# A decoder step on one core: two scattered stores on another queue, a head norm on VectorE, earlier gathers and weight splits, and memory scores three steps ahead

## The chip, the core and the metric

The kernel runs on one core of one Trainium2 chip. The core has a matrix engine (TensorE, PE in the profile), a vector engine (VectorE, DVE), an activation engine (ScalarE, ACT), a general engine (GpSimd, POOL) and an engine that here only issues transfers (SyncE, SP). Each engine works through its own queue in order. SP, ACT and POOL can each issue DMA transfers; the profile calls the issuing side SPq, ACTq, POOLq. Operands lie in SBUF; PE writes its sums to PSUM, which has eight banks of 128 x 512 floats.

The metric is the time on the device of one execution, in microseconds. The kernel before took 1546.40, 1548.47 and 1551.26 us in three runs, 1548.47 us in the median.

## The reference: what is computed

One layer of a hybrid decoder for a prompt of 1024 tokens and for 8 single sample tokens with their caches, all in float32 and width 1024:

```python
hp = rmsnorm(xp, norm_mix[l])
qa, ka, va, qr, kr, vr, gr = project(hp, w_in[l])
oa = diff_attention_prompt(qa, ka, va, rel_bias, lam)
s_p, o_r = retention_prompt(rotary(qr, pos_p), rotary(kr, pos_p) * kr_scale, vr, lg)
xp = xp + merge_groups(oa, o_r, gr, subln_a[l], lam_init) @ w_out[l]
mk_p, mv_p = mem_kv(mem_prompt, norm_mem_kv[l], w_mk[l], w_mv[l])
xp = xp + mem_attend(rmsnorm(xp, norm_mem_q[l]), mk_p, mv_p, w_mq[l], w_mo[l])
xp = xp + sq_relu_mlp(rmsnorm(xp, norm_mlp[l]), w_up[l], w_down[l])
...
k_past = cache_k[l][page_table].reshape(Bd, past, H_A, 2 * DK_A)
oa_d = diff_attention(qa_d, k_all, v_all, pos_d, kpos_d, rel_bias, lam)
```

Four heads of differential attention are each divided by their own root mean square (`head_rms`) before the output projection; four retention heads are run in chunks of 128 tokens. The memory attention has four heads of width 256 over 256 memory tokens. The sample tokens take the same path, with keys and values gathered from pages of a cache.

## The kernel before, in words

Every product of two float32 matrices is made of three matmuls, on a high part and a low part of each operand (high x high, high x low, low x high). A weight "unit" of 128 x 1024 is loaded by SP into a ring of three raw buffers (`raw`, L103), its high part is a cast on ACT (`wh`, L109) and its low part a subtraction on DVE or POOL (`wl`, L110). Activations are held transposed in `UH` and `UL` (high and low), 8 row tiles by 1032 columns (1024 prompt tokens and 8 sample tokens).

The order of the work is set by three things. The program is written in the order of its stages. A planner then orders each engine's queue by that program order and by when it believes an instruction's inputs are ready. And `pin` holds PE to the written order where it is set, while `issue_after(x)` puts instructions behind instruction x on x's engine.

The stages, with the stretch of the profile that each takes:

- To 56 us: the retention queries and keys (`qkp`, 8 PSUM banks at once), and the factors 1/rms of the 1032 tokens (`rstd`, a power on POOL, L121). L219 and L220 store these factors to a row in DRAM (`rrow`), one 4-byte element at a time, 1032 of them. ACT then takes the eight banks out (`qk`, L320), and the retention values (`vrp`) begin. Their weights are four units (`raw_u`, split into `vrw` for the first two).
- To 250 us: retention, chunk by chunk, and the attention values `va`. What one chunk leaves is turned into an operand by `pend()`, that is `to_operand`: four transposes on PE (`trR`), a cast, a subtraction and two stores. The last chunk's `pend()` runs at t = 0 of the loop over `va`.
- To 455 us: the attention heads, a loop over g, ten steps a head (x = g mod 10). A step has one `turn` (transposes `trA` of the weights `e`, L70), one `weigh` (L67) and, at some x, `scores` of later tiles; projections of the next head (`qkp`) fill PE's queue as long as there are any, and after them the sample tokens' scores (`dsc`) on gathered cache pages (`ck`, an indirect DMA of POOL, L577, into the same ring of three raw buffers). The norm of a finished head h-1 is spread over later steps: `norm_sums` at x = 2, `norm_factors` at x = 3 (column sums `ct`, three small products, and the power on POOL), `norm_send` at x = 4, `norm_row` at x = 5 (transpose `hrT`, a store and a broadcast load `rbh`), `norm_out` at x = 7: for heads 0 and 1 four products of 128 x 256 on POOL (L828) and a store, for head 2 one product on DVE (L831).
- To 566 us: the output projection `pr_o` over pairs (ft, c) through seven PSUM banks, with the gathered cache values of the sample tokens accumulated on DVE beside it (`dacc`, L1218). `fetch(2)` and `fetch(3)`, at (3,0) and (4,1), ask for weight units 4 to 7 (`who`, `wlo`); each also loads two rows of the residual.
- To 700 us: the memory queries (`mq`), the first two heads of memory keys (`mk`, taken out by L1395, `mko`) and the memory values (`mv`). Keys and values go to DRAM and come back as one unit a head (`raw_kv`, `wh_kv`, `wl_kv`).
- To 775 us: the memory attention, a loop over t of 16 pairs of query tiles, four a head. Step t has `scores` of pair t+2 (`ms`; a minimum `mmn` L1463 on DVE, two exponentials L1467 on ACT, a reciprocal, two scalings `me` L1471 on DVE), `weights` of pair t+1 (transposes `mtr`, cast `mph` L1482 on ACT, subtraction `mpl` L1483 on DVE) and `values` of pair t (`mpv`; cast `UH` L1501 on ACT, subtraction `UL` L1502 on DVE). The keys of heads 2 and 3 are PE's filler in it (`mk_units`, `mem_keys`, 48 matmuls each). Banks: `sp` 3, `pv` 2, `tr` 1, and two for the filler.
- To 1551 us: the memory output projection, the up projection and the down projection, both by a seven-product scheme. The change does not touch them.

Of the kernel before, what the change touches and what calls it, by code (L numbers as in the profile page):

```python
# [2 lines left out]

# [7 lines left out]
F32 = mybir.dt.float32  # L11
# [8 lines left out]
P = 128  # L20
D = 1024
NT = 1024
ND = 8
T = NT + ND
# [24 lines left out]
def decoder_step(ctx: ExitStack, tc: tile.TileContext, i: dict, o: dict):  # L49
    nc = tc.nc  # L50
# [110 lines left out]
    seen = {}  # L161
    s_ps = ExitStack()
    PS0 = s_ps.enter_context(pool("s_ps", space=PSUM))
    with pool("s") as A:
# [54 lines left out]
        nc.sync.dma_start(rrow[0:1, :NT].rearrange("a (t p) -> p (a t)", p=P), rstd1[:, :8])  # L219
        nc.sync.dma_start(rrow[0:1, NT:].rearrange("a p -> p a"), rstd1[:8, 8:9])  # L220


        lp = A.tile([P, 4, 64], F32, tag="lp", name="lp")
# [16 lines left out]
    with pool("a") as A:  # L240
# [267 lines left out]
        for t in (8, 0, 1, 2, 3, 4, 5, 6, 7):  # L508
            if t == 4:

                opd = [PS.tile([P, 512], F32, tag="op", name=f"opd_{x}", bufs=2) for x in range(2)]
                for p in range(2):
                    for x in range(2):
                        mm(opd[x][:4, :], hsel[:, p, :], wvs[p][:, 4 * x : 4 * x + 4, :], p == 0, p == 1)
                od = A.tile([P, 8, P], F32, tag="sn", name="od").rearrange("p s v -> p (s v)")[:4, :]
                for x in range(2):
                    nc.scalar.copy(od[:, x * 512 : x * 512 + 512], opd[x][:4, :])
                nc.sync.dma_start(ord_, od.rearrange("h (s v) -> h s v", s=8))
                odt = A.tile([P, 512], F32, tag="t1", name="odt", bufs=2)
                nc.sync.dma_start(odt[:8].rearrange("s (h v) -> s h v", h=4), ord_[:, :, :].rearrange("h s v -> s h v"))  # L520
                head_norm_gate(odt, gate_d, 8, 8, gate_d)
            if t == 0:
                with tc.issue_after(seen["PE"]):
                    pend()
            if t == 6:
                with tc.issue_after(seen["PE"]):
                    to_operand(gate_d, 8, 8, "d")
            ps, n = tokproj(units, t, f"vap_{t}", PS) if t < 8 else (decproj(units, f"vap_{t}", PS, vdec[:8]), 8)
            seen["PE"] = nc.cur_bb.bb.instructions[-1]
            v = vdec if t == 8 else A.tile([P, 512], F32, tag="gate", name=f"va_{t}", bufs=2)  # L530
            nc.scalar.activation(v[:n], ps[:n], AF.Copy, scale=rstd1[:n, t : t + 1])
            nc.sync.dma_start(o["v_p"][t * P : t * P + n, :] if t < 8 else o["v_s"], v[:n])
# [69 lines left out]
    with pool("b") as A:  # L602
# [171 lines left out]
        def norm_factors(h, sq):  # L774
# [48 lines left out]
        def norm_out(h):  # L823
            oraw, rbh = oraws[h], rows[h]
            if h < 2:
                for x in range(4):
                    xs = slice(x * 256, x * 256 + 256)
                    nc.gpsimd.tensor_mul(oraw[:, xs], oraw[:, xs], rbh[:, xs])  # L828
                nc.sync.dma_start(OP[h, :, :NT], oraw)
            else:  # L830
                nc.vector.tensor_mul(oraw, oraw, rbh)  # L831
                split_gain(oraw, subln8, h, 0, NT, gcol=0)
# [183 lines left out]
        for g in range(-4, 40):  # L1016
# [37 lines left out]
            if h > 0:  # L1054
# [54 lines left out]
    def proj_residual(A, bank, base, ktorder, xsrc, xdst, ssum, nm, us0, steps, when, parts, ahead=0, early=None, stage=()):  # L1109
# [167 lines left out]
    with pool("d") as A:  # L1277
# [97 lines left out]
        def head_kv(h):  # L1375
# [5 lines left out]
                     o["mv"][:, h * 256 : h * 256 + 256].rearrange("(x p) v -> p x v", p=P)),  # L1381
                ]

            KV[h] = unit_of(kv, f"kv{h}", lo_engine=nc.gpsimd if h else None)

        def mem_keys(pr, ps, us):
            for f in range(2):
# [8 lines left out]
                mo.rearrange("p (f m) -> p f m", f=2), ps.rearrange("p (f m) -> p f m", f=2),  # L1396
                rmb.unsqueeze(1).to_broadcast([P, 2, 256]),
            )
            nc.sync.dma_start(
                o["mkT"][pr * 256 : pr * 256 + 256, :].rearrange("(f p) m -> p f m", p=P), mo.rearrange("p (f m) -> p f m", f=2))  # L1400

# [47 lines left out]
        def scores(h, tp):  # L1449
            qh, ql = QS[h]  # L1450
            kvh, kvl = KV[h]
            sp = PS.tile([P, 2, 256], F32, tag="sp", name=f"ms_{h}_{tp}", bufs=3)
            for x in range(2):
                tk = slice((2 * tp + x) * P, (2 * tp + x) * P + P)
                mm3(
# [3 lines left out]
                        for f in range(2)  # L1459
                    ],  # L1460
                )
            mn = A.tile([P, 2], F32, tag="mmn", name=f"mmn_{h}_{tp}", bufs=2)
            nc.vector.tensor_reduce(mn, sp, AX.X, ALU.min)  # L1463
            sm = A.tile([P, 2], F32, tag="msm", name=f"msm_{h}_{tp}", bufs=2)
# [9 lines left out]
        def weights(h, tp):  # L1474
# [5 lines left out]
            ph = A.tile([P, 512], F32R, tag="mph", name=f"mph_{h}_{tp}", bufs=2)  # L1480
            pl = A.tile([P, 512], F32R, tag="mpl", name=f"mpl_{h}_{tp}", bufs=2)
            nc.scalar.copy(ph, tr)  # L1482
            nc.vector.tensor_sub(pl, tr, ph.bitcast(F32))  # L1483
# [33 lines left out]
        head_q(0)  # L1517
        us_mo = []
        pin[0] = True
        for t in range(-2, 16):  # L1520
            if t == -2:
                us = mk_units(2, None)
                fill = mem_keys(2, PD.tile([P, 512], F32, tag="mk", name="mk_2", bufs=1), us)
            if t == -1:
                head_kv(1)
                head_q(1)
            if t == 3:
                us = mk_units(3, nc.gpsimd)
                fill = mem_keys(3, PD.tile([P, 512], F32, tag="mk", name="mk_3", bufs=1), us)
            if t == 4:  # L1530
                head_kv(2)
                head_q(2)
            if t == 8:
                head_q(3)
            if t == 9:
# [8 lines left out]
            if t == -1:  # L1544
# [8 lines left out]
            if t in (2, 7):  # L1553
                for _ in fill:
                    pass
            if t in (14, 15):
# [658 lines left out]
```

## Time and profile before

| | before |
|---|---|
| median of three runs | 1548.47 us |
| the profiled execution | 1553.3 us |
| its span, first to last instruction | 1551.5 us |
| mean granted TensorE clock | 0.988 |
| PE busy | 1494.2 us, 96% |
| DVE busy | 1072.6 us, 69% |
| ACT busy | 651.0 us, 42% |
| POOL busy | 440.8 us, 28% |

The profiled execution is 4.8 us above the median. Several views of it are used below. The list of waits gives, for an engine and a line, what it stood idle for, the idle time in total, how often, and the longest. The table of stretches gives an engine's busy time and number of instructions in a stretch, then the granted clock of TensorE (1.00 is full), the share of the DMA engines that was busy, and GB/s. The timeline gives start, length, engine, line, operation, what it writes from what it reads, shapes and count, and behind them in brackets the idle time before it and what ended it. The chain of waits follows the work that ended last back through whatever released each piece. A tile's own view gives for each line the shortest, middle and longest duration in ns and the first and the last start in us. Matmuls are pipelined, so a busy PE is not PE at its peak, but an idle PE is idle.

### The profile page before, as it was taken

What the parts mean: (1) busy time and instruction counts of PE and PEld (TensorE: products, weight loads), DVE (VectorE), ACT (ScalarE), POOL (GpSimd) and SP (SyncE); (2) the same over time, 40 slices, a digit from 0 to 9 for tenths busy, and PEclk for the clock granted to TensorE, in tenths of its full rate; (3) what the DMA queues carried; (4) which work ended last, traced back from release to release, by engine and by line L of the source; (5) the groups of instructions that cost most, each with busy time, mean ns of one, the idle gap of its engine ahead of it and who ended that gap; (6) DMA issues with size and microseconds to landing.
All of it is one profiled execution on the core that took longest, in us unless ns stands there. A gap on an engine that the chain in (4) does not pass through costs nothing.

```text
span 1551.5 us, 26774 instructions
## 1 busy us (share of the span) xinstructions
PE 1494.2 (96%) x10483; PEld 1394.0 (90%) x10483; DVE 1072.6 (69%) x2096; ACT 651.0 (42%) x1267; POOL 440.8 (28%) x461
## 2 busy tenths in 40 slices
PE   9899999999999899999999899999999899999997
PEld 7678869999759899988899899999999799999996
DVE  4324513988865735566696988888788688787887
ACT  6323323665642332046634643333334444334454
POOL 0343302122533421124222234443335402020360
PEclk9999999999999999999999999999999999999999
DMA  8645334212766156451583334434335873636313
GB/s 291 171 116 156 78 104 115 82 51 69 235 215 240 48 202 180 138 183 64 182 269 129 101 138 151 151 138 150 137 138 172 293 232 86 197 82 198 96 42 110
DMA packets 121874, 230.02 MB, mean 148 GB/s; under 512 B 14209, under 2 KB 74480, under 8 KB 121620
## 3 DMA queue, kind: packets, MB, share of 16 engines
q1 hardware_dynamic: 91508, 170.30, 35.3%
q0 software_dynamic: 21024, 41.10, 8.6%
q10 hardware_dynamic: 9216, 16.91, 2.9%
q8 instruction: 82, 1.34, 0.4%
q14 instruction: 44, 0.36, 0.1%
HBM read 168.93 MB, written 57.52 MB: 146 GB/s over the span
## 4 chain that ended last, share of the span: by engine, by line
PE 63%; DVE 17%; DMA 11%; ACT 4%; issue 3%; POOL 1%; SPq 0%; DVEq 0%; ACTq 0%; POOLq 0%
PE dn L1928 17%; PE Z L1778 5%; PE mq L67 5%; PE pr_o L67 4%; PE qkp L67 4%; PE Y L1778 4%; PE vrp L67 3%; PE vap L67 3%; DVE wu L1617 3%; PE grp L67 3%; DMA raw_up<-in_wall 3%; PE X L1778 2%; PE pr_m L67 2%; PE sp L67 2%; PE av L67 2%
## 5 line engine op out<-in xcount | busy, mean ns | idle before, releaser
L1928 PE MATMUL dn<-UH,wd 128*128 128x258 f32 x1792 | 326.1, 284 | 7.7 <-ACT wd L1906 4.3
L1928 PEld LDWEIGHTS dn<-UH,wd 128*128 128x128 f32 x1792 | 278.2, 190 | 9.2 <-ACT wd L1906 4.7
L1928 PE MATMUL dn<-UL,wd 128*128 128x258 f32 x896 | 253.3, 283 | 0.0
L1928 PEld LDWEIGHTS dn<-UL,wd 128*128 128x128 f32 x896 | 169.7, 189 | 0.1
L1804 ACT ACTIVATE hq<-r 128x258 f32<-128x258 f32 x128 | 53.5, 419 | 162.8 <-DVE r L1803 162.8
L2008 DVE TENSOR_TENSOR c<-c,dn 128x258 f32<-128x258 f32 x216 | 88.4, 418 | 35.5 <-PE dn L1928 33.4
L1778 PE MATMUL Z<-T_h,wu 128*128 128x258 f32 x512 | 100.0, 287 | 7.0 <-DVE u L1828 5.3
L1906 ACT CAST wd<-raw_d 128x512 fp32r<-128x512 f32 x96 | 58.9, 618 | 102.6 <-PE dn L1928 84.5
L1617 DVE TENSOR_TENSOR wu<-raw_up,wu 128x512 fp32r<-128x512 f32 x96 | 92.0, 959 | 9.2 <-ACT wu L1616 9.2
L1778 PE MATMUL X<-UH,wu 128*128 128x258 f32 x512 | 97.7, 282 | 0.4 <-ACT p L1825 0.4
L110 DVE TENSOR_TENSOR wl_u<-raw_u,wh_u 128x1024 fp32r<-128x1024 f32 x46 | 59.8, 1308 | 50.9 <-ACT wh_u L109 49.0
L1778 PEld LDWEIGHTS Z<-T_h,wu 128*128 128x128 f32 x512 | 81.4, 189 | 10.4 <-DVE u L1828 8.3
L1907 DVE TENSOR_TENSOR wd<-raw_d,wd 128x512 fp32r<-128x512 f32 x96 | 75.5, 790 | 14.3 <-ACT wd L1906 14.2
L1778 PEld LDWEIGHTS X<-UH,wu 128*128 128x128 f32 x512 | 81.3, 188 | 0.7 <-ACT p L1825 0.7
L1900 DVE TENSOR_TENSOR UL<-raw_h,UH 128x1032 fp32r<-128x1032 f32 x56 | 77.3, 1381 | 6.4 <-ACT UH L1899 6.4
L109 ACT CAST wh_u<-raw_u 128x1024 fp32r<-128x1024 f32 x50 | 52.3, 1050 | 69.9 <-PE mq L67 43.2
L1899 ACT CAST UH<-raw_h 128x1032 fp32r<-128x1032 f32 x56 | 58.8, 1055 | 52.0 <-PE dn L1928 30.9
L1810 POOL TENSOR_TENSOR ht<-hq 128x258 f32<-128x258 f32 x32 | 22.3, 698 | 202.1 <-ACT hq L1804 188.1
L1920 POOL TENSOR_TENSOR raw_d<-raw_d,raw_d 128x512 f32<-128x512 f32 x16 | 23.3, 1456 | 179.5 <-DVE raw_d L1916 164.0
L1778 PE MATMUL Z<-T_l,wu 128*128 128x258 f32 x256 | 72.3, 282 | 0.0
L1778 PE MATMUL X<-UL,wu 128*128 128x258 f32 x256 | 72.3, 282 | 0.0
L1616 ACT CAST wu<-raw_up 128x512 fp32r<-128x512 f32 x96 | 57.1, 610 | 30.4 <-DVE raw_up L1623 23.7
(482 smaller groups left out, 4634.6 us busy)
## 6 DMA issues: line engine op xcount, KB each, us to landing
raw_u<-in_wall SPq DMA_DIRECT2D x59, 512.0 KB
HT<-ht POOLq DMA_DIRECT2D x32, 516.0 KB
raw_h<-HT SPq DMA_DIRECT2D x32, 516.0 KB
raw_up<-in_wall SPq DMA_DIRECT2D x32, 512.0 KB
raw_d<-in_wall SPq DMA_DIRECT2D x26, 512.0 KB
HQ<-hq ACTq DMA_DIRECT2D x32, 387.0 KB
raw_h<-HQ SPq DMA_DIRECT2D x24, 516.0 KB
cmk<-in_cmk SPq DMA_DIRECT2D x16, 512.0 KB
```

The lines of the kernel that those rows point to most:

```text
L67: pinned(nc.tensor.matmul(out, l, r, start=start, stop=stop))
L110: (lo_engine or nc.vector).tensor_sub(wl[:, :n], raw[:, :n], wh[:, :n].bitcast(F32))
L1616: nc.scalar.copy(w[:, :512], src)
L1617: nc.vector.tensor_sub(w[:, 512:], src, w[:, :512].bitcast(F32))
L1778: pinned(nc.tensor.matmul(ps, l, r[:, k, :], start=first and k == 0 and x == 0, stop=k == 3 and x == 2, skip_group_check=True))
L1804: nc.scalar.activation(h[:, PLACE[quad], :], r, AF.Square)
L1899: nc.scalar.copy(h, rv)
L1900: nc.vector.tensor_sub(l, rv, h.bitcast(F32))
L1906: nc.scalar.copy(w[:, :512], src)
L1907: nc.vector.tensor_sub(w[:, 512:], src, w[:, :512].bitcast(F32))
L1928: pinned(nc.tensor.matmul(ps, l, r[:, k, cq], start=first and k == 0 and x == 0, stop=k == 3 and x == 2, skip_group_check=True))
L2008: nc.vector.tensor_add(y, y, ps)
```

## The change

It has these parts:

1. The two stores of `rstd` into `rrow` are issued by ACT in place of SP.
2. The last chunk's `pend()` runs at t = 1 of the `va` loop in place of t = 0.
3. For heads 0 to 2 the power (`rsqrt_small`: one small DVE instruction and one on POOL) moves from `norm_factors` into `norm_send`, one step later, in front of the product that reads it; head 3 keeps it. `norm_out` of heads 0 and 1 is two products of 128 x 512 on DVE in place of four of 128 x 256 on POOL, and it runs at x = 9 in place of x = 7; head 2's stays at x = 7.
4. `fetch(2)` and `fetch(3)` of the output projection are at (1,1) and (2,1) in place of (3,0) and (4,1).
5. In the memory attention the scores run three steps ahead in place of two, so the loop begins at t = -3. `sp` becomes four tags of one bank each and `pv` has one bank in place of two; six tiles that nothing uses fix the order of the banks. The small tiles `mmn` and `msm` have three buffers in place of two. Loads of `raw_kv` are issued as before, but head 1's cast waits for the first `mph`, and its low part is made on DVE in place of POOL. The split of the first filler units is put behind the product `mko`. The calls for later heads and the filler move by one step, and the filler's counts per step change: 10, 18 and 22 at t = -2, -1, 0, where it was 10 and 12 at t = -1 and 12 at each of t = 0, 1, 2.

```diff
-        nc.sync.dma_start(rrow[0:1, :NT].rearrange("a (t p) -> p (a t)", p=P), rstd1[:, :8])
-        nc.sync.dma_start(rrow[0:1, NT:].rearrange("a p -> p a"), rstd1[:8, 8:9])
+        nc.scalar.dma_start(rrow[0:1, :NT].rearrange("a (t p) -> p (a t)", p=P), rstd1[:, :8])
+        nc.scalar.dma_start(rrow[0:1, NT:].rearrange("a p -> p a"), rstd1[:8, 8:9])
...
-            if t == 0:
+            if t == 1:
                 with tc.issue_after(seen["PE"]):
                     pend()
...
-            rsqrt_small(c8[:, 3, :], c8[:, 2, :], 8, 1.0 / P)
+            if h == 3:
+                rsqrt_small(c8[:, 3, :], c8[:, 2, :], 8, 1.0 / P)
             return c8

         def norm_send(h, c8):
             with tc.issue_after(seen["DVE"]):
+                rsqrt_small(c8[:, 3, :], c8[:, 2, :], 8, 1.0 / P)
                 nc.vector.tensor_mul(c8[:, 3, :], c8[:, 3, :], c8[:, 0, :])
...
-                for x in range(4):
-                    xs = slice(x * 256, x * 256 + 256)
-                    nc.gpsimd.tensor_mul(oraw[:, xs], oraw[:, xs], rbh[:, xs])
+                for x in range(2):
+                    xs = slice(x * 512, x * 512 + 512)
+                    nc.vector.tensor_mul(oraw[:, xs], oraw[:, xs], rbh[:, xs])
...
-                if x == NORM_AT[3]:
+                if x == NORM_AT[3] + 2 * (h < 3):
...
-            if (ft, c) in ((3, 0), (4, 1)):
-                fetch(2 if ft == 3 else 3)
+            if (ft, c) in ((1, 1), (2, 1)):
+                fetch(ft + 1)
...
-            KV[h] = unit_of(kv, f"kv{h}", lo_engine=nc.gpsimd if h else None)
+            raw = G.tile([P, T], F32, tag="raw", name=f"raw_kv{h}", bufs=3)
+            for dst, s in kv(raw):
+                nc.sync.dma_start(dst, s)
+
+            with tc.issue_after(seen["mph"]) if h == 1 else nullcontext():
+                KV[h] = unit_of(None, f"kv{h}", lo_engine=nc.gpsimd if h > 1 else None, raw=raw)
...
+        for tag in ("sp0", "sp1", "pv", "tr", "sp2", "sp3"):
+            PS.tile([P, 512], F32, tag=tag, name=f"{tag}_order", bufs=1)
...
-            sp = PS.tile([P, 2, 256], F32, tag="sp", name=f"ms_{h}_{tp}", bufs=3)
+            sp = PS.tile([P, 2, 256], F32, tag=f"sp{tp}", name=f"ms_{h}_{tp}", bufs=1)
...
-            pv = PS.tile([P, 2, 256], F32, tag="pv", name=f"mpv_{h}_{tp}", bufs=2)
+            pv = PS.tile([P, 2, 256], F32, tag="pv", name=f"mpv_{h}_{tp}", bufs=1)
...
-        for t in range(-2, 16):
-            if t == -2:
-                us = mk_units(2, None)
+        for t in range(-3, 16):
+            if t == -3:
+                with tc.issue_after(seen["DVE"]):
+                    us = mk_units(2, None)
...
-            if t + 2 < 16:
-                scores(*divmod(t + 2, 4))
+            if t + 3 < 16:
+                scores(*divmod(t + 3, 4))
...
+            if t == -1:
+
+                head_kv(1)
+                head_q(1)
...
-            for _ in range(12 if t in (-1, 0, 1, 2) else 18 if t in (4, 5, 6) else 0):
+            for _ in range(18 if t in (-1, 3, 4, 5) else 22 if t == 0 else 0):
                 next(fill, None)
```

More of the change, by code (lines that the diff above doesn't have):

```diff
@@ L1 @@
-from contextlib import ExitStack
+from contextlib import ExitStack, nullcontext
 from itertools import chain
@@ L1398, in mem_keys @@
             )
+            seen["DVE"] = nc.cur_bb.bb.instructions[-1]
             nc.sync.dma_start(
@@ L1461, in scores @@
                 )
-            mn = A.tile([P, 2], F32, tag="mmn", name=f"mmn_{h}_{tp}", bufs=2)
+            mn = A.tile([P, 2], F32, tag="mmn", name=f"mmn_{h}_{tp}", bufs=3)
             nc.vector.tensor_reduce(mn, sp, AX.X, ALU.min)
-            sm = A.tile([P, 2], F32, tag="msm", name=f"msm_{h}_{tp}", bufs=2)
+            sm = A.tile([P, 2], F32, tag="msm", name=f"msm_{h}_{tp}", bufs=3)
             e = A.tile([P, 2, 256], F32, tag="me", name=f"me_{h}_{tp}", bufs=2)
@@ L1482, in weights @@
             nc.scalar.copy(ph, tr)
+            seen["mph"] = nc.cur_bb.bb.instructions[-1]
             nc.vector.tensor_sub(pl, tr, ph.bitcast(F32))
@@ L1519, in decoder_step @@
         pin[0] = True
-        for t in range(-2, 16):
-            if t == -2:
-                us = mk_units(2, None)
+        for t in range(-3, 16):
+            if t == -3:
+                with tc.issue_after(seen["DVE"]):
+                    us = mk_units(2, None)
                 fill = mem_keys(2, PD.tile([P, 512], F32, tag="mk", name="mk_2", bufs=1), us)
[L1524 to L1527, printed above, removed]
+            if t == 2:
                 us = mk_units(3, nc.gpsimd)
                 fill = mem_keys(3, PD.tile([P, 512], F32, tag="mk", name="mk_3", bufs=1), us)
-            if t == 4:
+            if t == 3:
                 head_kv(2)
                 head_q(2)
+            if t == 7:
+                head_q(3)
             if t == 8:
-                head_q(3)
-            if t == 9:
                 head_kv(3)
@@ L1539, in decoder_step @@
                 ps_mo = [PD.tile([P, 512], F32, tag=("mk", "dt")[c], name=f"pr_m_0_{c}", bufs=1) for c in range(2)]
-            if t + 2 < 16:
-                scores(*divmod(t + 2, 4))
+            if t + 3 < 16:
+                scores(*divmod(t + 3, 4))
             if t in (13, 14):
                 out_part(0, 3 * t - 39)
-            if t == -1:
+            if t == -2:
                 for _ in range(10):
@@ L1548, in decoder_step @@
                 weights(*divmod(t + 1, 4))
+            if t == -1:
+                head_kv(1)
+                head_q(1)
             if t >= 0:
                 values(*divmod(t, 4))
-            for _ in range(12 if t in (-1, 0, 1, 2) else 18 if t in (4, 5, 6) else 0):
+            for _ in range(18 if t in (-1, 3, 4, 5) else 22 if t == 0 else 0):
                 next(fill, None)
-            if t in (2, 7):
+            if t in (1, 6):
                 for _ in fill:
```

## The prediction

> **What bounds the kernel now.** I read the busy times first, then what TensorE (PE) waits for, then the stretches behind those waits.
>
> ```profile
> PE 1494.2 (96%) x10483; PEld 1394.0 (90%) x10483; DVE 1072.6 (69%) x2096; ACT 651.0 (42%) x1267; POOL 440.8 (28%) x461
> ...
> PE vrp L260 <- ACT qk L320: 5.5, 1, 5.5
> PE trA L70 <- DVE e L735: 4.8, 3, 3.0
> PE pr_o L67 <- DVE wlo L110: 4.5, 1, 4.5
> PE mtr L70 <- DVE me L1471: 4.0, 3, 2.0
> PE dsc L67 <- DMA ck<-in_cache_kT,idk: 2.7, 1, 2.7
> PE mtr L70 <- DVE mpl L1483: 2.3, 1, 2.3
> PE ms L67 <- DVE mko L1395: 1.3, 1, 1.3
> PE trR L70 <- ACT vdec L272: 1.1, 1, 1.1
> ...
> 56.68:63.51 6.83, 3.58 (x9) 2.26 (x10) 2.76 (x3) 6.78 (x11) 0.47 (x1) 0.50 0.43 152
> 405.30:423.10 17.80, 14.69 (x79) 11.93 (x77) 17.43 (x57) 11.84 (x31) 11.38 (x14) 0.81 0.92 299
> 411.67:418.49 6.82, 5.76 (x23) 5.33 (x24) 6.61 (x23) 5.23 (x13) 4.36 (x5) 0.50 0.91 290
> 452.63:456.04 3.41, 3.41 (x11) 1.89 (x10) 1.18 (x5) 0.59 (x1) 0.00 (x0) 0.50 0.26 37
> 517.48:520.89 3.41, 3.41 (x14) 3.41 (x13) 2.71 (x5) 1.71 (x4) 2.71 (x4) 0.50 0.48 154
> 759.83:763.24 3.41, 3.41 (x17) 3.41 (x17) 2.21 (x5) 1.78 (x6) 0.00 (x0) 0.50 0.35 125
> ```
>
> PE is busy 96%, and the change removes none of its products: a gain is PE's idle time, or PE time at a lower clock. The waits listed are those at places that the change touches, 26.2 us in all. The stretches (length; busy PE, PEld, DVE, ACT, POOL; granted clock; DMA share; GB/s) show that behind five of them the clock is 0.50. Work done there would take half as long, so half of PE's busy time comes on top: 1.8, 2.9, 1.7, 1.7 and 1.7 us. Idle and slow clock together, 36 us, are the most that can be had.
>
> The sum is made against the profiled execution, 1553.3 us, 4.8 above the median of 1548.47; I take the difference off the median.
>
> **Part 1, the stores of `rstd`.**
>
> ```profile
> 33.20 0.43 SPq L103 DMA_DIRECT2D raw_u<-in_wall  x1
> 39.08 0.39 SPq L219 DMA_DIRECT2D rrow<-rstd  x1
> ...
> 41.43 0.43 SPq L103 DMA_DIRECT2D raw_u<-in_wall  x1
> ...
> 38.44 1.05 ACT L109 CAST vrw<-raw_u 128x1024 fp32r<-128x1024 f32 x1
> 46.05 0.69 ACT L320 ACTIVATE qk<-qkp,rstd 128x512 f32<-128x512 f32 x1 [6.56 <-PE qkp L67]
> 54.78 1.04 ACT L109 CAST vrw<-raw_u 128x1024 fp32r<-128x1024 f32 x1 [8.04 <-DMA raw_u<-in_wall]
> 55.73 4.15 ACT L320 ACTIVATE qk<-qkp,rstd 128x512 f32<-128x512 f32 x7
> ```
>
> SP issues nothing from 33.63 to 39.08, where it stands at the first store until `rstd` is there. The second `vrw` load goes out behind the stores at 41.43 and has landed at 54.78, 13.35 us later, while the one issued at 33.20 was there by 38.44, in 5.24. ACT waits 8.04 for it with seven of the eight `qk` banks queued behind, and PE has no bank: 5.5, and 1.8 of slow clock. After, SP goes past: the load leaves about 5 us sooner, at 36, ahead of the scattered elements (39), and should land by 42. On ACT the two issues (0.39 for the first) lie in its 6.56 idle; behind them there is only the cast, then `qk`. Next late is PE itself. Ends: 0 (the load is still held by the elements) and -7.3; I take **-6**, near the row of the undisturbed load, less some of the clock.
>
> The rule to weigh: the Trainium skill, DMA: Bandwidth & Descriptors, "Issuing engines are not separate DMA queues", says that transfers started by different engines share the same 16 DMA engines and interleave, so another issuer saves only the issue time. By it alone the sum would be 6 us less favourable; the trace supports sharing (13.35 against 5.24), but not that the order stays as it was.
>
> **Part 2, `pend()`.** At t = 0 the transposes `trR` wait 1.1 for ACT with the next products behind them; at t = 1 eight of them cover it. **-1**; ends 0 and -1.1.
>
> **Part 3, the head norm.**
>
> ```profile
> 360.88 2.88 POOL L828 TENSOR_TENSOR oraw<-oraw,rbh 128x256 f32<-128x256 f32 x4 [3.29 <-DMA rbh<-hrow]
> 408.13 3.33 POOL L828 TENSOR_TENSOR oraw<-oraw,rbh 128x256 f32<-128x256 f32 x4 [1.73 <-DMA rbh<-hrow]
> ...
> L831 DVE TENSOR_TENSOR oraw<-oraw,rbh x1: 1210/1210/1210, 459.7 to 459.7; 128x1024 f32<-128x1024 f32 x1
> ...
> 364.82 0.50 DVE L676 TENSOR_TENSOR Q<-qraw,Q 64x336 fp32r<-64x336 f32 x1
> 408.94 1.93 DVE L676 TENSOR_TENSOR Q<-qraw,Q 64x336 fp32r<-64x336 f32 x2
> 412.56 1.01 POOL L577 DMA_INDIRECT ck<-in_cache_kT,idk  x1 [0.30 <-issue]
> 425.99 1.07 PE L67 MATMUL dsc<-ck,qblkd 128*64 128x512 f32 x2
> 443.17 3.54 POOL L121 TENSOR_TENSOR c<-c,half 128x8 f32<-128x8 f32 x1
> ...
> POOL KA L668 <- ACT KA L667: 38.1, 6, 10.9
> ```
>
> In 405.30 to 423.10 DVE is busy 17.43 of 17.80 us, and the 3.0 gap at `trA` lies there. While POOL multiplies, the two `Q` products take 1.93 on DVE instead of 2 x 0.50: 0.9 to win, and some on their neighbours. But DVE gets 2 x 0.6 = 1.2 for each of two heads (half of L831's 1.21 for each product). Two steps later (47 us between the two heads, ten steps: 4.7 a step) this falls at about 417, still in the crowded stretch; the store of `OP` that follows it on SP slips as far, and is read back only for the output projection's operand (L957). Net: **-0.5**. Ends: -5.9 (gap and clock gone) and +3 (the two heads' 2.4 and a power's wait all on the path).
>
> The `rbh` of head 1 sits in the raw ring, and the gather at 412.56 follows its release. Two steps, 9.4 us, later it would be issued near 422, against a first use of that ring's later tiles at 425.99; a gather's data takes some microseconds. This can cost 0 to +9.4; I take 0 here, since other slots carry the first tiles, and make it a rival.
>
> In `norm_send` DVE's product now stands directly behind the power on POOL (1.66 to 3.54 long), with the `e` scalings behind it on DVE and PE's `trA` behind these. Queued behind on DVE are the reciprocals and `sp` scans of the next turn as well. Where POOL is not held, the wait is under 3.5 and lies in DVE's own idle outside the crowded stretch.
>
> **Also in part 3, head 2's power and the last gather.** POOL has the 3.54 power in front of the second half of the last gather, and PE then waits 2.7 (`dsc`), with 1.7 of slow clock. Moved behind the gather, the power costs its 3.54 to the row of factors instead, whose consumer comes at 459.7 (L831). Ends -4.4 and +3.5; **-2.5**, nearest the gap itself.
>
> **Part 4, weight units 4 to 7.**
>
> ```profile
> 486.69 1.17 SPq L103 DMA_DIRECT2D raw_u<-in_wall  x2
> 499.69 1.03 ACT L109 CAST who<-raw_u 128x1024 fp32r<-128x1024 f32 x1
> 512.76 2.18 DVE L1218 SCALAR_TENSOR_TENSOR dacc<-cv,at,dacc 128x128 f32<-128x128 f32 x8
> 515.28 1.51 DVE L110 TENSOR_TENSOR wlo<-raw_u,who 128x1024 fp32r<-128x1024 f32 x1
> ```
>
> The last unit's load was issued by 488 and its cast done at 500.7, but its subtraction stood in DVE's queue behind groups of `dacc` (one is shown) until 515.28: PE waits 4.5, and 1.7 of clock. Asked for several pairs sooner, the subtraction gets in front of several groups. SP's queue at that place holds the loads of the residual rows, which move along, and nothing that PE waits for; ahead of each load stands a free buffer of the ring, which the earlier unit's own subtraction must give back. So what moves surely is the place in DVE's queue, not the arrival. `dacc` slips by 1.5, with the seven PSUM banks of `pr_o` as cover, the same cover that today holds PE until 512. Ends 0 (DVE's order stays) and -6.2; **-5**, the gap and a little clock.
>
> **Part 5, the memory attention.**
>
> ```profile
> 703.41 1.04 ACT L109 CAST wh_kv<-raw_kv 128x1024 fp32r<-128x1024 f32 x1 [3.08 <-DMA raw_kv<-out_mkT]
> 740.71 0.28 PE L67 MATMUL mpv<-mph,wl_kv 128*128 128x256 f32 x1
> 741.14 0.58 ACT L1501 CAST UH<-mpv 128x512 fp32r<-128x512 f32 x1
> 742.27 0.68 DVE L1502 TENSOR_TENSOR UL<-mpv,UH 128x512 fp32r<-128x512 f32 x1
> 742.60 0.37 PE L67 MATMUL mpv<-mph,wh_kv 128*128 128x256 f32 x1
> ```
>
> The six order tiles issue no instruction, and the third buffers of `mmn` and `msm` only lift a wait. The split behind `mko` frees `ms` from it (1.3): so far the filler's subtractions stand ahead of it on DVE. Putting head 1's cast behind the first `mph` ends the 2.3 wait: ACT stood 3.08 for the load ahead of that cast. What is late next there is `me`, some 0.5: -3. The three waits on `me` at the later steps (4.0 and 1.7 of clock) go, since a step more lies between scores and transposes: -5.7. Against it stands the single `pv` bank: a group's last product ends at 740.99, `UL` has read the bank at 742.95, 1.96 later, and the next group began 742.60 - 740.99 = 1.61 later. That is 0.35 a step; about nine of the 16 steps have no filler: +3.2. Sum **-5** with 0.5 off for DVE's added low part (L110's time on POOL was free). Ends: -9.3, and +4 (3.2, 0.5 and a little) if the earlier scores gain nothing.
>
> **The sum.** -6 - 1 - 0.5 - 2.5 - 5 - 5 = -20 from 1553.3, 1533.3; on the median's footing **1528.5**.
>
> **A rule on the clock.** The Trainium skill, TensorE: Matmul & The Clock Gate, Part 1, says the clock is halved after at least one idle window of about 3.4 us, counted by a free-running window. The stretches of 3.41 and 6.82 agree with the window, but here 0.50 also follows gaps of 2.0, 2.7 and 3.0. By that rule the 1.7 each of `dsc` and `mtr` would not depend on those gaps and the sum would be -16.6; the rows decide, and I keep it.
>
> **The rivals.** 0.3%, 4.6 us, is about what a measurement tells from no change.
>
> - R1: the elements of `rrow` hold the load still, because the load leaves SP behind them or lands with them (13.35 against 5.24). Part 1 gives 0: 1534.5. For it: the engines are shared. Against: 5.1 us of head start. Chance 0.12.
> - R2: the memory loop is paced by the one `pv` bank: part 5 gives +4 in place of -5: 1537.5. For it: 1.96 against 1.61. Chance 0.15.
> - R3: the late gather: part 3 gives +9.4 more, 1538. Against it: only if the ring's other two slots don't bridge it. Chance 0.10.
> - R4, the other side: DVE's product in `norm_send` waits for a power that stands behind POOL's copies of `KA`, which themselves wait for ACT, up to 10.9 us. Three heads: +32.7, **1561**. It is slower than before by 4.6 from (20 + 4.6)/3 = 8.2 us a head. For it: POOL's order is the planner's, and the step behind the power's old place holds such copies. Against: DVE must be the bound at the time. Chance 0.10.
> - R5, the change does little: DVE, 17.43 of 17.80 in one stretch, or ACT shifts each gap to its next instruction and a fifth of the sum is left: 1544.5. Chance 0.08.
>
> **How the numbers follow.** The forecast has 0.45, its own range 1520 to 1535. Low 1514: all best ends together, -34. High 1546: beyond it lie R4 and half of R5's spread, under 0.2 together. Faster by over 4.6: forecast, R1 to R3 = 0.82; within 4.6: R5 in part, 0.07; slower: R4 and a little of R5, 0.11.
>
> **What would show it.** Part 1: the wait of `vrp` on `qk` is gone, no 0.50 behind 56, the second `vrw` cast near 42 to 46. Part 2: no `trR` wait. Part 3: L676 at 0.50 throughout, a DVE wait on POOL `c` under 3.5 a head (R4: 8 or more), both halves of the last gather ahead of the power, no new `dsc` wait (R3). Part 4: the last `wlo` before 510. Part 5: no `mtr` wait; R2 shows as `mpv` waiting on `UL`, some 0.35 each. Gaps of the same length at neighbouring lines would make the prediction wrong.

## The result, and the profile after

The changed kernel took 1537.01 us in the median of five runs, beside 1548.23 for the kernel before: a ratio of 0.9927, 95% interval 0.9900 to 0.9954. That is 11.2 us faster, inside the range, in the forecast direction, and little more than half of the 20 us forecast. Beside the kernel before on another chip it took 1545.29 against 1553.9, ratio 0.9948 (0.9928 to 0.9969). The profiled execution took 1537.01 us, its span is 1535.3, and its mean granted clock 0.994.

From the page of the changed kernel, then its list of waits (what PE stood idle for: total, times, longest):

```profile
PE 1490.1 (97%) x10483; PEld 1390.7 (91%) x10483; DVE 1069.7 (70%) x2101; ACT 653.0 (43%) x1267; POOL 430.8 (28%) x452
...
PE sp L67 <- DVE mn L719: 3.6, 2, 2.9
PE vrp L67 <- ACT vr L346: 2.9, 1, 2.9
PE dsc L67 <- DMA ck<-in_cache_kT,idk: 2.3, 1, 2.3
PE trA L70 <- DVE e L735: 2.0, 2, 1.7
...
PE mpv L67 <- DVE UL L1514: 1.3, 2, 1.1
PE av L67 <- DVE VL L695: 1.2, 1, 1.2
```

The waits on `qk`, `wlo`, `me`, `mpl`, `mko` and `vdec` are gone. The wait at `dsc` is still there. The largest new waits are `vrp` on another eviction (L346), the scores on `mn`, and `mpv` on `UL`.

Since PE is never idle for long, the times at which its products start cut the span into stages. This table is made from the tiles' own views (first and last start of their products), in us, one execution of each kernel. The untouched stages show how much of a difference is the spread between executions.

| stage of PE's products | before | changed | difference |
|---|---|---|---|
| start to last `vrp` | 109.6 | 109.0 | -0.6 |
| to first `sp` (part 2) | 161.3 | 160.0 | -1.3 |
| to first `pr_o` (attention, part 3) | 186.5 | 186.7 | +0.2 |
| to last `pr_o` (part 4) | 106.5 | 100.2 | -6.3 |
| to last `mq` (untouched) | 94.7 | 94.6 | -0.1 |
| to first `pr_m` (memory, part 5) | 105.9 | 98.3 | -7.6 |
| to last `dn` (untouched) | 775.8 | 775.2 | -0.6 |

In these two executions two parts gave nearly everything, part 1's head start was gone by the end of its stage, and the attention gave nothing.

### The profile page after: what moved, and what is told of

Its sections match the earlier page's. It is cut to its first block, busy times and chain, and to the rows that moved or that the text cites. A ratio compares the mean times of both kernels' runs of the same rounds, so it can differ in the third digit from the quotient of the medians.

```text
span 1535.3 us, 26765 instructions
## 1 busy us (share of the span) xinstructions
PE 1490.1 (97%) x10483; PEld 1390.7 (91%) x10483; DVE 1069.7 (70%) x2101; ACT 653.0 (43%) x1267; POOL 430.8 (28%) x452
## 4 chain that ended last, share of the span: by engine, by line
PE 71%; DVE 11%; DMA 6%; ACT 3%; issue 3%; POOL 2%; SPq 0%; DVEq 0%; ACTq 0%; POOLq 0%
PE dn L1942 18%; PE Z L1792 7%; PE pr_o L67 6%; PE Y L1792 5%; PE mq L67 5%; PE X L1792 4%; PE qkp L67 4%; PE vap L67 3%; PE grp L67 3%; PE sp L67 2%; PE pr_m L67 2%; PE vrp L67 2%; PE av L67 1%; PE mpv L67 1%; DMA raw_up<-in_wall 1%
## 5 line engine op out<-in xcount | busy, mean ns | idle before, releaser
L110 DVE TENSOR_TENSOR wl_u<-raw_u,wh_u 128x1024 fp32r<-128x1024 f32 x46 | 58.6, 1279 | 56.2 <-ACT wh_u L109 54.1
```

Source lines behind the costliest of these rows:

```text
L110: (lo_engine or nc.vector).tensor_sub(wl[:, :n], raw[:, :n], wh[:, :n].bitcast(F32))
```

## The experiments

All kernels below are edits of the changed kernel unless it says otherwise. The stage times are read as in the table.

### Each part undone alone

**The stores back on SP.**

```diff
-        nc.scalar.dma_start(rrow[0:1, :NT].rearrange("a (t p) -> p (a t)", p=P), rstd1[:, :8])
-        nc.scalar.dma_start(rrow[0:1, NT:].rearrange("a p -> p a"), rstd1[:8, 8:9])
+        nc.sync.dma_start(rrow[0:1, :NT].rearrange("a (t p) -> p (a t)", p=P), rstd1[:, :8])
+        nc.sync.dma_start(rrow[0:1, NT:].rearrange("a p -> p a"), rstd1[:8, 8:9])
```

> The changed kernel with the two stores of rstd back on SP; all else as changed. Theory A (what the two traces show): the first vrp product starts 3 to 4 us later than in the changed kernel, with the 5.5 us wait on qk and the slow clock back, but the 2.9 us wait of vrp on vr (L346) disappears, since that eviction stands behind a POOL addition that ends near 83 us in both traces; the last vrp product ends within 1 us of the changed kernel's, and the time is 0 to 2 us above the changed kernel's. Theory B (the prediction's term): the head start is kept to the end, and the time is about 6 us above the changed kernel's.

The first `vrp` product came at 60.9 in place of 56.2, the last at 111.6. The wait on `qk` was back with 6.4 us and the one on `vr` was gone: one takes the place of the other.

```profile
PE vrp L260 <- ACT qk L320: 6.4, 1, 6.4
```

The last product is 2.6 us later than in the changed kernel, where theory A had it within 1 us and theory B needs about 6. The time, 1544.1 us, is 0.9937 (0.9912 to 0.9961) of the kernel before, on the chip of the next three runs; the changed kernel was not timed beside them, so the totals don't decide between the theories. The runs of the next section do.

**The head norm back.** Power at x = 3, products of heads 0 and 1 on POOL at x = 7.

```diff
-                for x in range(2):
-                    xs = slice(x * 512, x * 512 + 512)
-                    nc.vector.tensor_mul(oraw[:, xs], oraw[:, xs], rbh[:, xs])
+                for x in range(4):
+                    xs = slice(x * 256, x * 256 + 256)
+                    nc.gpsimd.tensor_mul(oraw[:, xs], oraw[:, xs], rbh[:, xs])
...
-                if x == NORM_AT[3] + 2 * (h < 3):
+                if x == NORM_AT[3]:
```

> The changed kernel with the head norm as before: power one step earlier, the product of heads 0 and 1 on POOL in four pieces and two steps earlier. Theory A: the attention stage (first score to first product of the output projection) has the same length within 1 us: POOL's products slow DVE's Q products from 0.5 to about 1 us each, but the 1.4 us of products on DVE come off DVE's queue in the same crowded stretch; the wait at dsc stays 2.3 to 2.7 in both. Theory B (the prediction): the stage gets 3 us longer, 2.5 of them at dsc.

The attention stage took 185.6 us, 1.1 less than the changed kernel's 186.7 (186.4 to 189.3 in seven executions of that code), and the wait at `dsc` stood at 2.8. The time was 1536.62 us, 0.9890 (0.9861 to 0.9919) of the kernel before: without part 3 the kernel is no slower. Theory B is out; theory A is nearly met. DVE's timeline, first of the changed kernel, then of this one, shows both halves of theory A: without POOL's products the two `Q` products took 1.04, with them 1.93; but the norm's products now stand in DVE's own queue, between the `e` and `mn` on which PE waits.

```profile
406.31 1.04 DVE L676 TENSOR_TENSOR Q<-qraw,Q 64x336 fp32r<-64x336 f32 x2
...
410.55 0.69 DVE L830 TENSOR_TENSOR oraw<-oraw,rbh 128x512 f32<-128x512 f32 x1
411.15 0.61 DVE L735 SCALAR_TENSOR_TENSOR e<-e,mn,e 128x384 f32<-128x384 f32 x1
411.68 0.16 DVE L733 RECIPROCAL mn<-sm 128x1 f32<-128x1 f32 x1
411.75 0.67 DVE L830 TENSOR_TENSOR oraw<-oraw,rbh 128x512 f32<-128x512 f32 x1
```

```profile
402.30 1.93 DVE L676 TENSOR_TENSOR Q<-qraw,Q 64x336 fp32r<-64x336 f32 x2
```

**The fetches back** at (3,0) and (4,1).

```diff
-            if (ft, c) in ((1, 1), (2, 1)):
-                fetch(ft + 1)
+            if (ft, c) in ((3, 0), (4, 1)):
+                fetch(2 if ft == 3 else 3)
```

> The changed kernel with the two fetches of the output projection back at (3,0) and (4,1). Theory A: the wait of pr_o on wlo is back with 4 to 5 us, the output projection ends 6 to 6.5 us later than in the changed kernel, and the total is 6 us longer. Theory B: the 6.3 us by which this stage was shorter in the changed trace came with the earlier stages (other gather and norm times move DVE's queue), and undoing the fetches costs less than 3 us.

The output projection took 107.3 us in place of 100.2, and `pr_o` waited for `wlo` again. The rows of `wlo`'s subtractions, of the changed kernel and of this one, with the wait, show where the last of the four stood (last start): 504.6 against 514.1. The time was 1548.14 us, 0.9969 (0.9951 to 0.9987) of the kernel before. For the stage theory A holds; the changed kernel was not timed beside this one.

```profile
L110 DVE TENSOR_TENSOR wlo<-raw_u,who x4: 1212/1218/1227, 482.3 to 504.6; 128x1024 fp32r<-128x1024 f32 x4
```

```profile
L110 DVE TENSOR_TENSOR wlo<-raw_u,who x4: 1216/1220/1501, 482.7 to 514.1; 128x1024 fp32r<-128x1024 f32 x4
...
PE pr_o L67 <- DVE wlo L110: 4.7, 1, 4.7
```

**The memory attention back** to two steps ahead.

```diff
-        for t in range(-3, 16):
+        for t in range(-2, 16):
...
-            if t + 3 < 16:
-                scores(*divmod(t + 3, 4))
+            if t + 2 < 16:
+                scores(*divmod(t + 2, 4))
...
-            pv = PS.tile([P, 2, 256], F32, tag="pv", name=f"mpv_{h}_{tp}", bufs=1)
+            pv = PS.tile([P, 2, 256], F32, tag="pv", name=f"mpv_{h}_{tp}", bufs=2)
```

> The changed kernel with the memory attention as before (two steps ahead, two pv banks, first split on POOL, first filler split not held). Theory A: from the first score to the last product of the memory output projection the stage gets 7 us longer, with the waits at ms (1.3), mtr on mpl (2.3) and mtr on me (4.0) back and the two waits of mpv on UL (1.3) gone. Theory B (the prediction's term): 5 us.

From the last `mq` product to the first `pr_m` it took 103.0 us, against 98.3 to 99.3 in the kernels with the new loop and banks and 105.9 in the kernel before. Its waits:

```profile
PE mtr L70 <- DVE me L1473: 4.0, 3, 2.1
PE mtr L70 <- DVE mpl L1485: 0.8, 1, 0.8
```

The three waits on `me` are the same as before; of the two waits at the start of the loop only 0.8 of 3.6 came back. The time was 1546.52 us, 0.9947 (0.9918 to 0.9976) of the kernel before. Against this run the new loop is worth some 4 us, theory B's size rather than theory A's; the other 3 had to be looked at in the kernel before itself.

**The kernel before, once more.**

> The kernel before once more, for a second look at its stages. Theory A (the stages of the first profile are typical): last vrp product at 108 to 112 us, 106.5 us of output projection, 105 to 107 from the last mq product to the first of the memory output projection, with the waits at ms (1.3) and mtr on mpl (2.3). Theory B: the 2.9 us by which the kernel with the memory attention undone was shorter there than this kernel's first profile is the spread of a transfer's landing, and the stage comes out at 103 to 105.

The stage took 102.7, a little under theory B's 103, the waits at its start 0.6 (`mpl`) and none at `ms`; another run of that code, below, took 105.7. The wait on `mpl` goes with the landing of `raw_kv`, which holds ACT's cast:

```profile
702.33 1.05 ACT L109 CAST wh_kv<-raw_kv 128x1024 fp32r<-128x1024 f32 x1 [1.40 <-DMA raw_kv<-out_mkT]
```

ACT waited 1.40 here and 1.56 in the kernel with the loop undone, where PE's wait was 0.6 and 0.8; it waited 3.08 and 3.28 in the other two executions of the old code, where PE's was 2.3 and 2.5. Why the wait at `ms` comes and goes isn't shown. The change removes both where they occur: over the three runs of the kernel before's code the stage is 102.7 to 105.9, with the new one 98.3 to 99.3.

### Where part 1's head start went

SP's, ACT's and POOL's timelines of the changed kernel:

```profile
35.15 1.24 SPq L103 DMA_DIRECT2D raw_u<-in_wall  x2
...
41.45 0.39 ACTq L219 DMA_DIRECT2D rrow<-rstd  x1
...
43.30 1.99 ACT L109 CAST vrw<-raw_u 128x1024 fp32r<-128x1024 f32 x2
47.98 5.45 ACT L320 ACTIVATE qk<-qkp,rstd 128x512 f32<-128x512 f32 x8 [2.69 <-PE qkp L67]
...
69.94 0.69 ACT L346 ACTIVATE vr<-vrp,rstd 128x512 f32<-128x512 f32 x1 [0.16 <-PE vrp L67]
83.95 0.72 ACT L346 ACTIVATE vr<-vr,rstd 8x512 f32<-8x512 f32 x1 [13.33 <-POOL vr L273]
84.58 1.80 ACT L346 ACTIVATE vr<-vrp,rstd 128x512 f32<-128x512 f32 x3
...
82.48 1.44 POOL L273 TENSOR_TENSOR vr<-vr,vdec 8x512 f32<-8x512 f32 x1
```

The loads leave SP ahead of the stores, and ACT takes out all eight banks in one go. But behind the first eviction of `vrp`, ACT scales the eight sample rows, whose sum POOL makes (L273) in a queue full of the rotary products of `qk`. ACT waits 13.33 us with three full banks behind it. In the kernel before the same wait was 6.76 and ended at 82.73: PE was so late that it did not wait for it.

```profile
75.28 0.69 ACT L346 ACTIVATE vr<-vrp,rstd 128x512 f32<-128x512 f32 x1 [0.16 <-PE vrp L67]
82.73 0.72 ACT L346 ACTIVATE vr<-vr,rstd 8x512 f32<-8x512 f32 x1 [6.76 <-POOL vr L273]
```

PE's head start is handed to this wait.

**The changed kernel once more.**

> The changed kernel once more, beside the kernel before on the same chip. Theory A (the difference of the two profiles is the effect): 16 us faster, ratio 0.9895. Theory B (the difference of the medians is the effect): 11 us, ratio 0.9927. In the profile, the stage up to the last vrp product may end anywhere from 105 to 110 us, the wait of vrp on vr from 0.5 to 5 us, since the four kernels so far with the same code there gave that.

The median difference is 8.6 us, nearer theory B. In this execution the wait of `vrp` on `vr` was 6.4 us and the last `vrp` product came at 111.0. Over seven executions with this code up to there it came at 104.2 to 111.0, with waits of 0 to 6.4. POOL's sum of the sample rows ended at 80.4 where there was no wait and at 85.5 where it was 6.4. POOL begins this run of work when ACT has copied the sample rows of `qk` out (L272): at 63.04 in the kernel before, at 59.20 to 64.34 in these. In these seven that copy stands on ACT behind the casts of three weight units that SP asks for from 50 us on, so it moves with their landing.

**The sample rows' scaling behind the fourth eviction.**

```diff
-        scaled(8, vr[8], 8)
         for t in range(8):
             scaled(t, ps2[t] if t < 2 else tokproj(units, t, f"vrp_{t}", PS)[0], P)
+            with tc.issue_after(nc.cur_bb.bb.instructions[-1]): scaled(8, vr[8], 8) if t == 3 else None
```

> The changed kernel with the scaling of the eight sample rows of vr on ACT put behind the fourth eviction of vrp (it was behind the first), so that ACT no longer stands on POOL's addition with the banks of vrp full. Theory A: the wait of vrp on vr (0.5 to 5.0 us so far) is gone, no slow clock between 80 and 95 us, and the last vrp product is at 104 to 106 us in place of 105 to 110. Theory B: the banks are late for another reason (the products' own weights), the wait comes back at another line, and the last vrp product stays at 107 to 110.

ACT's timeline of this kernel: the evictions go on at PE's pace, and the sum is nearly there when ACT comes to it.

```profile
68.01 0.69 ACT L346 ACTIVATE vr<-vrp,rstd 128x512 f32<-128x512 f32 x1 [0.15 <-PE vrp L67]
69.40 0.69 ACT L346 ACTIVATE vr<-vrp,rstd 128x512 f32<-128x512 f32 x1 [0.70 <-PE vrp L67]
74.96 0.69 ACT L346 ACTIVATE vr<-vrp,rstd 128x512 f32<-128x512 f32 x1 [4.87 <-PE vrp L67]
80.52 0.69 ACT L346 ACTIVATE vr<-vrp,rstd 128x512 f32<-128x512 f32 x1 [4.87 <-PE vrp L67]
84.27 0.72 ACT L346 ACTIVATE vr<-vr,rstd 8x512 f32<-8x512 f32 x1 [3.06 <-POOL vr L273]
```

PE no longer waits at `vrp`, no slow clock is left in the stage, and the last `vrp` product comes at 102.3, 7.3 us before that of the kernel before. The time is 1539.31 against 1553.9, ratio 0.9909 (0.9876 to 0.9942); the changed kernel took 1545.29 on the same chip. Theory A holds, with a last product 2 us earlier than it said.

**The same edit in the kernel before.**

> The kernel before with only the scaling of the sample rows of vr moved behind the fourth eviction. Theory A: the two waits are in series, so without the earlier stores this gains nothing: the wait of vrp on qk (5.5) stands and the last vrp product stays at 108.5 to 110. Theory B: ACT's wait on POOL costs in the kernel before as well, and it comes 2 to 5 us earlier.

```profile
PE vrp L260 <- ACT qk L320: 4.9, 1, 4.9
```

The last `vrp` product came at 109.5, with `vrp` waiting 4.9 for `qk`: alone the edit gives nothing. The two waits are in series, and only both together give the 7 us.

### The attention stage

**Nearly no product.** Left out is the norm of heads 0 and 1 (one column of the product stays).

```diff
-                for x in range(2):
-                    xs = slice(x * 512, x * 512 + 512)
-                    nc.vector.tensor_mul(oraw[:, xs], oraw[:, xs], rbh[:, xs])
+                nc.vector.tensor_mul(oraw[:, :1], oraw[:, :1], rbh[:, :1])
```

> The changed kernel with the product of the norm's row left out for heads 0 and 1 but for one column (these heads go unscaled into the output projection): what the 2 x 1.4 us on DVE cost. Theory A: DVE is the bound in the crowded stretch, and without the product at 410 the wait of the scores on mn (2.9) shrinks to 1.5 or less and the attention stage gets 1.5 to 3 us shorter than the changed kernel's 186.7. Theory B: the product lies beside other work and the stage stays within 0.5 us.

The wait on `mn` shrank as theory A had it (3.6 in the changed kernel), but the waits on `e` grew by as much (2.0 in the changed kernel), and the stage took 187.8. That is 1.1 above the 186.7 that theory B meant to keep within 0.5, and at the mean of the executions with the product, 187.7: nothing was gained.

```profile
PE trA L70 <- DVE e L735: 4.8, 3, 2.2
...
PE sp L67 <- DVE mn L719: 0.9, 1, 0.9
```

So neither the products on DVE nor POOL's slowing of DVE sets this stretch; with either gone, PE waits about as long at another link (`e` in place of `mn`). What its true bound is was not settled.

**Head 2's power behind the last gather.** The forecast had the power move behind the gather. POOL's timeline of the changed kernel shows that it did not:

```profile
441.80 1.21 POOL L577 DMA_INDIRECT ck<-in_cache_kT,idk  x1 [2.43 <-PE dsc L67]
443.02 3.54 POOL L121 TENSOR_TENSOR c<-c,half 128x8 f32<-128x8 f32 x1
446.75 2.03 POOL L577 DMA_INDIRECT ck<-in_cache_kT,idk  x1 [0.19 <-issue]
```

One step later in the program is still ahead of the gather's second half in the planner's order of POOL's queue. This kernel puts head 2's power and row one step later again (and keeps the edit to the sample rows):

```diff
-                if x == NORM_AT[1] + 1:
+                if x == NORM_AT[1] + 1 + (h == 3):
                     todo.append(lambda: sqs.append(norm_send(h - 1, sqs.pop())))
-                if x == NORM_AT[2]:
+                if x == NORM_AT[2] + (h == 3):
                     todo.append(lambda: norm_row(h - 1, sqs.pop()))
```

> The changed kernel with the sample rows' scaling behind the fourth eviction, and with head 2's power and row one step later, so that POOL issues both halves of the last gather before the power. Theory A (the power between the halves makes PE wait): the wait of dsc (2.3 to 3.2) goes, L831's product still comes in time, and the attention stage is 2 to 4 us shorter than the 186.4 to 189.3 of the kernels with the same code there: 184 to 186. Theory B (the second half waits for its ring slot or the gather itself is the length): dsc waits as before and the stage stays.

Its POOL timeline:

```profile
435.64 1.20 POOL L577 DMA_INDIRECT ck<-in_cache_kT,idk  x1 [2.45 <-PE dsc L67]
437.15 2.54 POOL L577 DMA_INDIRECT ck<-in_cache_kT,idk  x1 [0.31 <-issue]
439.71 1.68 POOL L121 TENSOR_TENSOR c<-c,half 128x8 f32<-128x8 f32 x1
```

The wait at `dsc` is gone and the stage took 182.8 us, 3.6 to 6.5 less than the 186.4 to 189.3 of the kernels with the changed kernel's code there. `pr_o` waits 0.7 for head 2's operand in its place. The time is 1532.08 us against 1556.62, ratio 0.9854 (0.9808 to 0.9900).

**The same with the norm of heads 0 and 1 on POOL again.**

> The same, and with the norm of heads 0 and 1 as in the kernel before (power one step earlier, products on POOL, two steps earlier). Theory A (the change of the norm is worth nothing or costs a little): the attention stage is 0 to 2 us shorter than that of f_vr8_and_late_power, and the time about 15 to 18 us below the kernel before. Theory B (the product on DVE is the better one): 1 to 3 us longer.

The stage took 182.8 again, and the time is 1532.22 us, ratio 0.9853 (0.9813 to 0.9893). No difference between the norm on DVE and on POOL is seen; with one profile of each, and a stage that varies by 2.9 us between executions of the same code, one of a us or two isn't excluded. Both kernels are some 24 us below the kernel before, and below the changed kernel by the ratio as well (0.9854 and 0.9853 against 0.9927 and 0.9948), though on another chip.

### The banks of the memory attention

Three score banks in turn and two `pv` banks, three steps ahead:

```diff
-            sp = PS.tile([P, 2, 256], F32, tag=f"sp{tp}", name=f"ms_{h}_{tp}", bufs=1)
+            sp = PS.tile([P, 2, 256], F32, tag=f"sp{(4 * h + tp) % 3}", name=f"ms_{h}_{tp}", bufs=1)
...
-            pv = PS.tile([P, 2, 256], F32, tag="pv", name=f"mpv_{h}_{tp}", bufs=1)
+            pv = PS.tile([P, 2, 256], F32, tag=("pv", "pv2")[tp % 2], name=f"mpv_{h}_{tp}", bufs=1)
```

> The changed kernel with three score banks and two pv banks (as before) but three steps ahead. Theory A: the waits of mpv on UL (1.1 and 0.2) go and nothing comes in their place, since a score bank is free once its pair is scaled: the stretch from the last mq product to the first of the memory output projection is 97 us in place of 98.3 to 98.8. Theory B: the fourth score bank is what carries the third step ahead: the waits of mtr on me come back (up to 4.0) and the stretch gets 1 to 4 us longer.

Neither theory foresaw what came. The waits of `mpv` on `UL` went and none of `mtr` on `me` came, so in this run three score banks were enough. But the planner put the sample tokens' scores (`dtq_m` to `dbp_m`, a chain over PE, DVE and ACT) later and closer together, and PE stood at its last link:

```profile
PE dbp_m L67 <- DVE dsm_m L559: 5.3, 1, 5.3
```

The stage took 103.1, some 4 more than with one `pv` bank. Whether two `pv` banks with that chain in its old place would gain the 1.3 us wasn't tried.

## Why the prediction was right or wrong

The sum by its terms, with the old and the new code of each stage over all executions that have it (means; three of the kernel before's code, seven of the changed one's in the first, third and fifth row, where the fifth leaves out the two kernels with the later power):

| term | forecast | measured |
|---|---|---|
| part 1, to the last `vrp` | -6 | 110.0 to 107.9: -2.1 (with the sample rows moved: -7) |
| part 2 | -1 | 161.3 to 160.1: -1.2 |
| part 3, norm and last gather | -0.5 and -2.5 | 186.3 to 187.7: +1.4 |
| part 4 | -5 | 107.0 to 100.2: -6.8 |
| part 5 | -5 | 104.8 to 98.7: -6.1 |
| sum | -20 | -14.8 |

- Part 1: the mechanism held up to the end of `qk`. The load left SP at 35.15 with the one ahead of it, the second `vrw` cast was done at 45.3, and ACT took all eight banks from 47.98 on. R1 fell: the load went ahead of the elements. (The rule set beside it, of the Trainium skill, DMA: Bandwidth & Descriptors, "Issuing engines are not separate DMA queues", is not touched by that: what was saved is the load's wait in SP's queue, not a share of the engines.) The step that failed is "Next late is PE itself". Next late was ACT, standing on POOL's sum of the sample rows. The row that said so was in the trace of before: ACT's scaling at 82.73, behind 6.76 us of idle, starts 7.45 us after the eviction at 75.28; a head start had to reach it.
- Part 2 was right: the wait of `trR` is gone, and the stage is as short with the stores back on SP (160.1), so the gain isn't part 1's.
- Part 3, the norm: -0.5 can't be told from the spread; undoing it made the kernel no slower. What failed in it is "Two steps later this falls at about 417": head 1's products ran at 410.55, 4.2 us behind the `Q` products, where POOL's ran 0.8 us ahead of them, so some 5 us later and not 9.4. R3 did not occur: the gather that follows the ring's release went out at 412.70, and PE waited for none but the last. R4 did not either: DVE's longest wait on one of the moved powers was 1.6 us.
- Part 3, the gather: "Moved behind the gather" failed. The power was moved in the program and not in POOL's queue. That the power between the halves was the cause was right: with it really behind, the stage got shorter by 3.6 to 6.5 us, more than the 2.5 forecast and about the upper end, 4.4 (4.9 against the mean).
- Part 4 was right in mechanism and undersized by 1.8: with all of the slow clock the upper end, -6.2, would have been nearer.
- Part 5 was right in sign and within its ends. The `pv` bank was oversized: two waits, 1.3 us, in place of nine of 0.35. The 3.6 us at the loop's start are not a fixed price: executions of the old code show 0.6 to 3.6.
- The clock rule beside the sum: -16.6 takes 1.7 each for `dsc` and `mtr` off the -20, but the -2.5 for the gather is less than its gap of 2.7 and has no slow clock in it; by that rule it would be -18.3.
- The sum: parts 1 and 3 gave 8.3 us less than forecast and parts 2, 4 and 5 gave 3.1 more. In parts 1 and 3 the gap went to the next link, as R5 describes it for the whole; that the two partly cancel was luck, though the range, up to 1546, would have held the result without it. By stages the sum is -14.8, while the medians differ by 11.2 and 8.6. The stage up to `vrp` alone varies by 7 us between executions of the changed kernel, and the untouched stage behind the memory attention from 773 to 780; one profile per kernel can't be set against a median more exactly. Part of the difference is on record: the two profiled executions of the changed kernel have the highest granted clock of their sets (0.994 beside 0.990 to 0.992, and 0.992 beside 0.984 to 0.991), so these profiles show less slow clock than the timed runs have. Whether that is all of it is not settled.

## What to carry to other kernels

Before a gap is booked as gained, give the engine its head start in the trace and walk on to the next wait of each in-order queue on its path: a wait that costs nothing today (here ACT on POOL, at 82.73) is the one that takes the gain. A step moved in the program has moved only when the engine's queue shows it: read the order of the queue there. Where stages have different limits, compare the starts of the bound engine's products stage by stage, over several executions of the same code; a part that a median can't resolve shows there.

## What the runs showed of the hardware

The granted clock after a gap of PE is not a matter of the gap's length alone. Stretches right behind the wait at `dsc`, of the kernel before with the sample rows moved (gap 2.54) and of the changed kernel's second execution (gap 2.58); the granted clock is the third number from the end:

```profile
451.85:455.26 3.41, 3.41 (x14) 2.60 (x15) 1.76 (x6) 0.59 (x1) 0.00 (x0) 0.66 0.36 73
```

```profile
454.76:458.17 3.41, 3.27 (x20) 2.27 (x21) 2.00 (x6) 1.15 (x2) 0.00 (x0) 1.00 0.23 78
```

All 17 gaps of 3.0 us or more in these fourteen profiles were followed by a clock of 0.50 (up to 900 us); of those from 2.0 to 2.9 some were and some weren't, with the same code. The Trainium skill, TensorE: Matmul & The Clock Gate, Part 1, has an idle window of about 3.4 us that runs free; that it runs free agrees with this spread, but gaps well short of 3.4 us are enough here (2.05 before the `mtr` at 759.49 of the kernel before). For an estimate it means that a gap between 2 and 3 us carries its slow clock (up to 1.7 us) only at times, and that removing it gains that only at times.
